# One row at a time for the modulation sums of a fused encoder layer, and nine banks of partial products kept apart by ScalarE

## The chip, the cores and the metric

The kernel runs on one core of a Trainium2 chip. Its time is the device time of one execution in microseconds (us). Before the change three runs gave 939.26, 941.5 and 938.09 us; the median is 939.26 us. The profile comes from a further execution.

## The reference, cut to what matters

One layer (DEPTH is 1) of an encoder over 512 positions of width 2048, in float32:

```python
c_act = silu(c)                                        # 2048 values
mod = c_act @ w_ada + b_ada                            # w_ada is 2048 x 6144
shift, scale, gate = split(mod, 3)
h = rms_norm(x, g) * (1.0 + scale) + shift             # 512 x 2048
proj = h @ w_in                                        # w_in is 2048 x 7168
...                                                    # attention and retention heads on proj
out = y @ w_out
return rms_norm(x + gate * out, final_gain)
```

What matters here is the order that the data force: a column block of h can only be made when the whole 2048-row sum of w_ada for its shift and its scale columns is done, and a row block of w_in can only be multiplied when its column block of h is there.

## The kernel before, in words

**Precision.** Each product is made of three matmuls on halves. `conv` (L170 on) splits a loaded tile of weights: ScalarE casts the high half (L180), VectorE subtracts it to get the low half (L185), both into a tile `w` of three buffers. `mm3` (L94 to L97) then issues high x high, high x low and low x high. h is held the same way, as `hh` and `hl`, transposed (128 of its columns by 512 positions per k).

**The first phase** (L953 to L1032) makes 13 of the units of the projection, 256 columns each: q, k, v, z of the first three attention pairs and one more q. It doesn't wait for all of h. The 16 row blocks k of w_in are cut in six chunks, `CHUNKS = [1, 2, 2, 3, 4, 4]`; this text counts them from 1, so chunk 2 has k = 1, 2, chunk 3 has k = 3, 4, chunk 4 has k = 5, 6, 7, and chunk 5 has k = 8 to 11. In each chunk all 13 units are multiplied with the chunk's k. Two units (`persist`) stay in PSUM all along; of the 11 others each chunk's two banks (pool psA, three banks) are taken out and added up in SBUF: the first chunk by a copy of ScalarE (L992), the later ones by an add of VectorE (L994). In chunk 3 five banks (`MORE`) are copied to tiles of their own by ScalarE instead (L990), and added in chunk 5 (`add_more`, L936). The last unit of a chunk keeps its banks for the next chunk (`keep_now`).

**The modulation sums.** While a chunk is multiplied, the next chunk's columns of w_ada are loaded and summed (`ada_pieces`, L218). The rows come 128 at a time, 16 row blocks in all; a load brings as many of them as fit 2048 elements a partition into a tile `araw` of three buffers. The accumulator, one tile of tag `aacc`, is started by ScalarE with row block 0 (L239) and gets the 15 others by one VectorE instruction each (L243). Then `sums` (L250) transposes it on TensorE into the one bank of pool psM, ScalarE sums each column over the partitions (L278), and VectorE makes shift `sv` and scale `av`. `make_h` (L194) writes for each k the high half `hh` (L197) and the full value `ht` (L202, for chunk 2 on VectorE at L200), both from `xT[k]`; `make_hl` (L204) then subtracts (L211). The tile for `hl` of a chunk has the same tag as that chunk's `xT`, a single buffer, so the first `hl` of a chunk can be written when every `hh` and `ht` of the chunk has been made. `ht` has a tag of its own with four buffers; `aacc` has two.

**The order of the work** is written out by hand. One unit with at most two k is an item: 13 items a chunk for one or two k, 26 for three or four. Items are fed one by one; at feed f (from feed 19 on) the loads of item f are issued, the split of item f-8, and the matmuls and evacuations of item f-10. After each feed the pieces that `agenda` holds for it are issued. `plan` spreads the pieces of the next chunk's sums over the chunk's feeds, from three feeds after its first (`LAG`): first the steps, each of which adds one load's row blocks and starts another load, then `sums`, then each `make_h`, then each `make_hl`. So for chunk 5's sums, planned while chunk 4 is fed, the 20 pieces start at feed 42, the first addition (the fourth piece) at feed 45. The tile framework then orders the instructions of each engine by its own schedule, within the data and buffer dependencies and the extra orders that `after` gives, so pieces can run well ahead of the place where they are issued.

**The last rows of x.** Its 512 rows are normalised and transposed by four row groups. The last group's transposes (`last_rows`, L478) go through psM in four batches issued at feeds 10 to 13, the first taken out by ScalarE, the three others by VectorE (L391). Batches 2 to 4 are k = 5 and up.

Of the kernel before, what the change touches and what calls it, by code (L numbers as in the profile page):

```python
# [17 lines left out]
P = 128  # L18
D = 2048
S = 512  # L20
# [14 lines left out]
UC = 256  # L35
CHUNKS = [1, 2, 2, 3, 4, 4]
N_PERSIST = 2
MORE_AT, MORE = 2, 5
ADA_SPAN = 0.65
TAB_SPAN = 16  # L40
WARM = 4, 1, 1
FIRST_W = OFF_KA + UC
LAG = 3
RAW, RAW1, WB, LOOK, LEAD, LEAD0, LEAD1, EB, YB = 3, 3, 3, 2, 4, 2, 8, 1, 22


# [9 lines left out]
def trunk_kernel(ctx, tc, x, c, norm_gain, w_ada, b_ada, w_in, w_out, dec_f, dec_b, final_gain, out):  # L56
# [116 lines left out]
    def conv(src, n, at, pin_low=None):  # L173
        both = wp.tile([P, 1024 + 128], F32R, tag="w", name="w", bufs=WB)
        hi, lo = both[:, at : at + 512], both[:, at + 512 : at + 1024]
        dh, dl = hi[:, :n], lo[:, :n]
        if len(src.shape) == 3:
            dh = dh.rearrange("p (k f) -> p k f", k=src.shape[1])
            dl = dl.rearrange("p (k f) -> p k f", k=src.shape[1])
        c1 = nc.scalar.copy(dh, src)  # L180
        if pin_low is not None:
            pin_low.append(lambda: pin(nc.vector.tensor_tensor(dl, src, f32(dh), op=ALU.subtract)))
            pin(c1)
            return hi, lo
        c2 = nc.vector.tensor_tensor(dl, src, f32(dh), op=ALU.subtract)  # L185
        marks["split"] = c2
        marks["conv"] = marks.get("conv", 0) + 1
        if marks["conv"] < 3:
            after(c1, marks["hh"])
            after(c2, marks["hl"])  # L190
        return hi, lo


    def make_h(k, nk, k_first):  # L194
        tmp = aap.tile([P, S], F32, tag="ht", name="ht", bufs=4)
        a, b = av[:, k : k + 1], sv[:, k : k + 1]
        ins = nc.scalar.activation(hh[k], xT[k], AF.Identity, scale=a, bias=b)  # L197
        if k_first == 1:
            marks["hh"] = ins
            nc.vector.tensor_scalar(tmp, xT[k], a, b, op0=ALU.mult, op1=ALU.add)  # L200
        else:
            nc.scalar.activation(tmp, xT[k], AF.Identity, scale=a, bias=b)  # L202
        tmps[k] = tmp
# [11 lines left out]
    def h_pieces(k0, nk):  # L215
        return [(lambda f=f, k=k: f(k, nk, k0)) for f in (make_h, make_hl) for k in range(k0, k0 + nk)]

    def ada_pieces(k0, nk):  # L218
        n = nk * P
        acc = aap.tile([P, 2, 4 * P], F32, tag="aacc", name="aacc")  # L220
        npc = 2048 // (2 * n)

        raws = {}

        def load(kr):
            raw = aap.tile([P, 2048], F32, tag="araw", name="araw", bufs=AR)
            rv = raw[:, : npc * 2 * n].rearrange("p (a b f) -> p a b f", a=npc, b=2)
            src = wa[kr * P : (kr + npc) * P, 0 : 2 * D].rearrange(
                "(a p) (b f) -> p a b f", p=P, b=2
            )[:, :, :, k0 * P : k0 * P + n]  # L230
            for b in range(2):
                nc.sync.dma_start(rv[:, :, b], src[:, :, b])
            raws[kr] = rv

        def add(kr):
            rv = raws[kr]
            for a in range(npc):
                if kr + a == 0:
                    first = nc.scalar.activation(acc[:, :, :n], rv[:, a], AF.Copy, scale=ct[:, 0:1])  # L239
                    if k0 in (1, 3):  # L240
                        after(first, marks["hh"])
                else:
                    ins = nc.vector.scalar_tensor_tensor(  # L243
                        acc[:, :, :n], rv[:, a], ct[:, kr + a : kr + a + 1], acc[:, :, :n],
                        op0=ALU.mult, op1=ALU.add,
                    )
                    if k0 in (1, 3) and kr + a == 1:
                        after(ins, marks["hl"])

        def sums():  # L250
            ks = slice(k0, k0 + nk)
            sl = slice(NK + k0, NK + k0 + nk)
            if k0 == 1:
                ps = bank(psM, "psm")
                for b in range(2):
                    for j in range(nk):
                        nc.tensor.matmul(
                            ps[:, b * nk + j : b * nk + j + 1], acc[:, b, j * P : (j + 1) * P], ones[:, 0:1],
                            start=b + j == 0, stop=b + j == nk, skip_group_check=True,
                        )  # L260
                nc.vector.tensor_tensor(sv[:, ks], ps[:, 0:nk], bg[:, ks], op=ALU.add)
                nc.vector.tensor_tensor(av[:, ks], ps[:, nk : 2 * nk], bg[:, sl], op=ALU.add)
                marks["hl"] = nc.vector.tensor_tensor(
                    av[:, ks], av[:, ks], bg[:, 32 + k0 : 32 + k0 + nk], op=ALU.mult
                )
                return
            for b in range(2):
                if b == 0 or nk > 2:
                    ps = bank(psM, "psm")
                    o = 0  # L270
                for j in range(nk):
                    cs = slice(o + j * P, o + (j + 1) * P)
                    nc.tensor.transpose(ps[:, cs], acc[:, b, j * P : (j + 1) * P], ident)
                for j in range(nk):
                    junk = aap.tile([P, P], F32, tag="junk", name="junk")
                    col = b * NK + k0 + j
                    cs = slice(o + j * P, o + (j + 1) * P)
                    nc.scalar.activation(junk, ps[:, cs], AF.Identity, accum_out=md[:, col : col + 1])  # L278
                o += nk * P
            nc.vector.tensor_tensor(sv[:, ks], md[:, ks], bg[:, ks], op=ALU.add)  # L280
            nc.vector.tensor_tensor(av[:, ks], md[:, sl], bg[:, sl], op=ALU.add)
            nc.vector.tensor_tensor(av[:, ks], av[:, ks], bg[:, 32 + k0 : 32 + k0 + nk], op=ALU.mult)

        krs = list(range(0, NK, npc))

        def step(i):
            if i >= AR:
                add(krs[i - AR])
            if i < len(krs):
                load(krs[i])  # L290

        return (
            [(lambda i=i: step(i)) for i in range(len(krs) + AR)]
            + [sums]
            + h_pieces(k0, nk)
        )
# [87 lines left out]
    def evacuated(t, b, eng, late=False):  # L384
        k0, k1 = BANKS[b]
        for i, g in enumerate(groups):
            lo, hi = max(g[0], k0), min(g[-1] + 1, k1)
            if i and lo < hi:
                dst = xt_tiles[i][:, lo - g[0] : hi - g[0], t * P : (t + 1) * P]
                src = psx[t, b][:, (lo - k0) * P : (hi - k0) * P].rearrange("p (k f) -> p k f", k=hi - lo)  # L390
                marks[eng] = eng(dst, src)  # L391
                if not late:
                    pin(marks[eng])

    act, dve = nc.scalar.copy, nc.vector.tensor_copy
    hl[0] = hp.tile([P, 1, S], F32R, tag="g0", name="hl0")[:, 0, :]
    tmp0 = aap.tile([P, S], F32, tag="ht", name="ht", bufs=4)


    def h0_high(cols, src):  # L400
# [78 lines left out]
    def last_rows(b):  # L479
        if b == 1:  # L480
            v = xn[3][:, 1024:D]
            after(nc.vector.tensor_scalar_mul(v, v, rsx[:, 3:4]), marks["sc"])
        turned(3, b, True)
        evacuated(3, b, dve if b else act, True)

    late = [lambda b=b: last_rows(b) for b in range(4)]
    x_scope.close()
# [430 lines left out]
    agenda = {}  # L918
    fed = 0

    for i, f in enumerate(late):
        agenda.setdefault(LEAD1 + LOOK + i, []).append(f)

    def plan(fs, start, span):
        for i, f in enumerate(fs):
            agenda.setdefault(start + (i * span) // len(fs), []).append(f)
# [3 lines left out]
        x3_scope.close()  # L930
        pools["more"] = xn_scope.enter_context(tc.tile_pool(name="more", bufs=1, side="right"))

    agenda.setdefault(LEAD1 + LOOK + len(late), []).append(open_more)
    more = {}

    def add_more(u, i):  # L936
        nc.vector.tensor_tensor(accs[u][i], accs[u][i], more[u, i], op=ALU.add)

    def open_wk():
        xn_scope.close()  # L940
# [12 lines left out]
    for ci, nk in enumerate(CHUNKS):  # L953
# [19 lines left out]
        loose = [u for u in order if u >= N_PERSIST]  # L973
        kept, keep_now = keep_now, {} if lastc else {loose[-1]: None}
        if ci == MORE_AT:
            apart = [(u, i) for u in loose[1:-1:3] for i in range(2)][:MORE]
        if ci == MORE_AT + 2:
            plan([(lambda u=u, i=i: add_more(u, i)) for u, i in apart], fed + 1, 12)
        for u in order:
            mode, c0, ev = ph1[u]  # L980

# [33 lines left out]
        if not lastc:  # L1015
            n2 = CHUNKS[ci + 1]
            nxt = []
            for i in range(0, n2, 4):
                nxt += ada_pieces(k0 + nk + i, min(4, n2 - i))
            before_last = ci == len(CHUNKS) - 2  # L1020
            span = int(len(items) * ADA_SPAN) if before_last else len(items)
            plan(nxt, fed + LAG, span)
            if before_last:
                agenda.setdefault(fed + LAG + span, []).append(open_wk)
        if ci == 0:
# [358 lines left out]
```

## Time and profile before

| | us |
|---|---|
| median of three runs | 939.26 |
| the profiled execution | 940.26 |
| its span, first to last instruction | 938.5 |
| what lies around the span | 1.76 |
| TensorE busy | 920.0 |
| VectorE busy | 619.9 |
| ScalarE busy | 381.0 |

The profile has one line per group of instructions, with the engine, the operation, the tiles as out<-in and the time of one. PE is TensorE's matmuls, PEld its weight loads, DVE is VectorE, ACT is ScalarE, SPq the queue that issues most loads. "idle before" is time in which the engine did nothing before an instruction, with what released it. A windows view gives busy times of the engines for a stretch of the span, with the granted clock of TensorE and what the DMA moved. The chunks can be told apart in the trace by counting matmuls: a unit takes 12 of 128x512, or 24 of 128x256, for two k. Chunk 2 starts at 47.6 us of the span, chunk 3 at 87.1, chunk 4 at 126.9, chunk 5 at 182.8 and chunk 6 at about 255.

### The profile page before, as it was taken

The numbers are of one execution on the slowest core, as the hardware profiler recorded it, in microseconds if no ns is written. First come the engines' busy times: TensorE is split into PE (matmuls) and PEld (weight loads), VectorE is DVE, ScalarE is ACT, GpSimd is POOL, SyncE is SP. The second block draws the span as 40 slices with busy tenths as digits, with TensorE's granted clock in tenths as the row PEclk, the third lists the DMA queues.
The fourth block names the chain that finished last, engine by engine and source line by source line (L and its number), as shares of the span: only waits on it lengthen the run. The fifth ranks groups of instructions, "written<-read, shape, count | busy, mean of one in ns | idle before, by whom it ended". The sixth has DMA issues, their size and how long they took to land.

```text
span 938.5 us, 14336 instructions
## 1 busy us (share of the span) xinstructions
PE 920.0 (98%) x5578; PEld 807.9 (86%) x5578; DVE 619.9 (66%) x1096; ACT 381.0 (41%) x752; POOL 13.7 (1%) x25
## 2 busy tenths in 40 slices
PE   8999999999999999999999999999999999999996
PEld 5787788888988888988998899998899988888896
DVE  4899999959467886666675565845744382546554
ACT  4843525253254655444343232422343372324321
POOL 2000000000000000000000000000000000000001
PEclk9999999999999999999999999999999999999998
DMA  9987988524322222214444534434513148234305
GB/s 329 352 294 259 308 288 281 177 90 127 100 90 67 70 67 70 66 55 136 149 134 146 179 102 158 144 126 158 167 58 112 65 162 290 90 130 140 111 3 180
DMA packets 110244, 141.50 MB, mean 151 GB/s; under 512 B 5800, under 2 KB 81496, under 8 KB 109792
## 3 DMA queue, kind: packets, MB, share of 16 engines
q1 hardware_dynamic: 109072, 137.27, 44.6%
q10 hardware_dynamic: 1008, 3.28, 0.9%
q8 instruction: 44, 0.72, 0.3%
q14 instruction: 24, 0.20, 0.1%
q0 software_dynamic: 96, 0.03, 0.0%
HBM read 136.36 MB, written 4.20 MB: 150 GB/s over the span
## 4 chain that ended last, share of the span: by engine, by line
PE 84%; DVE 7%; DMA 4%; issue 2%; ACT 2%; POOL 0%; SPq 0%; POOLq 0%; DVEq 0%; ACTq 0%
PE pp L97 24%; PE pw L97 12%; PE pp L95 12%; PE po L97 12%; PE pw L95 6%; PE po L95 6%; DVE aacc L243 3%; PE op L97 3%; DMA araw<-in_w_ada_dram 2%; PE sp L97 2%; PE op L95 2%; PE tp L799 1%; DMA raw<-in_w_ada_dram 1%; DVE w L185 1%; PE sp L95 1%
## 5 line engine op out<-in xcount | busy, mean ns | idle before, releaser
L185 DVE TENSOR_TENSOR w<-raw,w 128x512 fp32r<-128x512 f32 (+1 forms) x288 | 193.6, 673 | 214.8 <-ACT w L180 214.5
L180 ACT CAST w<-raw 128x512 fp32r<-128x512 f32 (+1 forms) x289 | 174.7, 606 | 390.5 <-PE pp L97 187.1
L95 PE MATMUL pp<-w,hh 128*128 128x256 f32 x576 | 160.2, 278 | 0.0
L97 PE MATMUL pp<-w,hh 128*128 128x256 f32 x576 | 159.7, 277 | 0.0
L97 PE MATMUL pp<-w,hl 128*128 128x256 f32 x576 | 159.7, 277 | 0.0
L95 PEld LDWEIGHTS pp<-w,hh 128*128 128x128 f32 x576 | 108.4, 188 | 1.0 <-issue 0.2
L97 PEld LDWEIGHTS pp<-w,hh 128*128 128x128 f32 x576 | 108.3, 188 | 0.9
L97 PEld LDWEIGHTS pp<-w,hl 128*128 128x128 f32 x576 | 108.2, 188 | 0.0
L95 PE MATMUL pw<-hh,w 128*128 128x512 f32 x256 | 101.5, 397 | 3.4 <-DVE acc L994 2.1
L95 PE MATMUL pp<-hh,w 128*128 128x512 f32 x256 | 99.8, 392 | 0.4 <-DVE kl L699 0.4
L97 PE MATMUL pw<-hh,w 128*128 128x512 f32 x256 | 100.0, 391 | 0.1
L97 PE MATMUL pp<-hl,w 128*128 128x512 f32 x256 | 100.0, 391 | 0.0
L97 PE MATMUL pp<-hh,w 128*128 128x512 f32 x256 | 99.9, 390 | 0.0
L97 PE MATMUL pw<-hl,w 128*128 128x512 f32 x256 | 99.7, 391 | 0.0
L97 PE MATMUL po<-w,yh 128*128 128x512 f32 (+1 forms) x252 | 91.1, 361 | 0.0
L95 PE MATMUL po<-w,yh 128*128 128x512 f32 (+1 forms) x252 | 91.0, 361 | 0.0
L97 PE MATMUL po<-w,yl 128*128 128x512 f32 (+1 forms) x252 | 91.0, 361 | 0.0
L243 DVE SCALAR_TENSOR_TENSOR aacc<-araw,ct,aacc 128x512 f32<-128x512 f32 (+2 forms) x75 | 76.4, 1018 | 5.6 <-DMA araw<-in_w_ada_dram 2.9
L994 DVE TENSOR_TENSOR acc<-acc,pw 128x512 f32<-128x512 f32 x95 | 63.5, 686 | 4.6 <-PE pw L97 4.1
L95 PEld LDWEIGHTS pw<-hh,w 128*128 128x128 f32 x256 | 48.1, 188 | 17.2 <-DVE acc L994 4.7
L95 PEld LDWEIGHTS pp<-hh,w 128*128 128x128 f32 x256 | 48.0, 188 | 10.8 <-DVE kl L699 0.8
L97 PEld LDWEIGHTS pw<-hh,w 128*128 128x128 f32 x256 | 48.1, 188 | 10.6 <-DVE w L185 0.5
(237 smaller groups left out, 1568.6 us busy)
## 6 DMA issues: line engine op xcount, KB each, us to landing
raw<-in_w_in_dram SPq DMA_DIRECT2D x94, 512.0 KB, 3.6
araw<-in_w_ada_dram SPq DMA_DIRECT2D x48, 512.0 KB, 6.8
graw<-in_w_ada_dram SPq DMA_DIRECT2D x64, 256.0 KB, 3.0
raw<-in_w_out_dram SPq DMA_DIRECT2D x32, 512.0 KB, 3.7
raw<-in_w_in_dram SPq DMA_DIRECT2D x16, 384.0 KB, 4.1
araw<-in_w_ada_dram SPq DMA_DIRECT2D x16, 384.0 KB, 4.3
res<-in_x_dram SPq DMA_DIRECT2D x16, 256.0 KB, 6.2
raw<-in_w_in_dram SPq DMA_DIRECT2D x11, 256.0 KB, 5.1
```

The source lines that it names most:

```text
L95: nc.tensor.matmul(o, lh, rh, start=start, stop=False, skip_group_check=True)
L97: nc.tensor.matmul(o, a, b, start=False, stop=stop and b is (rl if swap else rh), skip_group_check=True)
L180: c1 = nc.scalar.copy(dh, src)
L185: c2 = nc.vector.tensor_tensor(dl, src, f32(dh), op=ALU.subtract)
L243: ins = nc.vector.scalar_tensor_tensor(acc[:, :, :n], rv[:, a], ct[:, kr + a : kr + a + 1], acc[:, :, :n], op0=ALU.mult, op1=ALU.add,)
L799: nc.tensor.transpose(tp_[:, j * P : (j + 1) * P], pt[:, j * P : (j + 1) * P], ident)
L994: nc.vector.tensor_tensor(accs[u][i], accs[u][i], ps[i], op=ALU.add)
```

## The change

It has five parts. In chunks 2 and 3 the pieces of the next chunk's sums are no longer spread evenly: each row block is a piece of its own (`row`), placed by a share of the chunk's items (`ENDS`), and each addition is ordered behind the split before the latest one issued (`marks["prev"]`). `ht` loses its tag: two `ht` share one tile of tag `aacc`, and the accumulator is asked for at its first addition. `MORE` goes from five banks to nine, one bank of each of nine units, and their adds in chunk 5 are spread over 27 feeds and ordered behind the latest split. The last rows of x go to feeds 10, 23, 25 and 27, and are all taken out by ScalarE. `tmp0`, a temporary of the first k, moves to the pool x3p.

```diff
-MORE_AT, MORE = 2, 5
+MORE_AT, MORE = 2, 9
+LATE = 10, 23, 25, 27
+ENDS = {1: (0.72, 0.86), 2: (0.68, 0.82)}
...
-        marks["split"] = c2
+        marks["prev"], marks["split"] = marks.get("split", c2), c2
...
     def make_h(k, nk, k_first):
-        tmp = aap.tile([P, S], F32, tag="ht", name="ht", bufs=4)
+        if (k - k_first) % 2 == 0:
+            tmps["pair"] = aap.tile([P, 2, 4 * P], F32, tag="aacc", name="ht")
+        tmp = tmps["pair"][:, (k - k_first) % 2, :]
...
-    def ada_pieces(k0, nk):
+    def ada_pieces(k0, nk, ends=None):
         n = nk * P
-        acc = aap.tile([P, 2, 4 * P], F32, tag="aacc", name="aacc")
+        accw = {}
...
-        def add(kr):
+        def add(kr, only=None):
             rv = raws[kr]
-            for a in range(npc):
+            for a in range(npc) if only is None else [only]:
+                if kr + a == 0:
+                    accw["t"] = aap.tile([P, 2, 4 * P], F32, tag="aacc", name="aacc")
+                acc = accw["t"]
...
+                    if only is not None:
+                        after(ins, marks["prev"])
...
+        def row(r):
+            add(krs[r // npc], r % npc)
+            if r % npc == npc - 1 and r // npc + AR < len(krs):
+                load(krs[r // npc + AR])
+        if ends:
+            n_items, rows_end, h_end = ends
+            at = [i - 5 for i in range(AR)] + [r * rows_end * n_items / NK - 0.5 for r in range(NK)]
+            fs = [lambda i=i: load(krs[i]) for i in range(AR)] + [lambda r=r: row(r) for r in range(NK)]
+            hs = h_pieces(k0, nk)
+            s = (rows_end + 0.04) * n_items
+            at += [s] + [s + 0.3 + (h_end * n_items - s) * j / len(hs) for j in range(len(hs))]
+            return list(zip(at, fs + [sums] + hs))
...
-    tmp0 = aap.tile([P, S], F32, tag="ht", name="ht", bufs=4)
+    tmp0 = x3p.tile([P, S], F32, name="ht0")
...
-        evacuated(3, b, dve if b else act, True)
+        evacuated(3, b, act, True)
...
-    for i, f in enumerate(late):
-        agenda.setdefault(LEAD1 + LOOK + i, []).append(f)
+    for at, f in zip(LATE, late):
+        agenda.setdefault(at, []).append(f)
...
     def add_more(u, i):
-        nc.vector.tensor_tensor(accs[u][i], accs[u][i], more[u, i], op=ALU.add)
+        after(nc.vector.tensor_tensor(accs[u][i], accs[u][i], more[u, i], op=ALU.add), marks["split"])
...
-            apart = [(u, i) for u in loose[1:-1:3] for i in range(2)][:MORE]
+            apart = [(u, 0) for u in loose[1 : 1 + MORE]]
-            plan([(lambda u=u, i=i: add_more(u, i)) for u, i in apart], fed + 1, 12)
+            plan([(lambda u=u, i=i: add_more(u, i)) for u, i in apart], fed + 1, 3 * MORE)
...
+            if ends:
+                for at, f in nxt:
+                    agenda.setdefault(fed + LEAD1 + LOOK + math.floor(at), []).append(f)
+            else:
+                plan(nxt, fed + LAG, span)
```

More of the change, by code (lines that the diff above doesn't have):

```diff
@@ L250, in sums @@
         def sums():
+            acc = accw["t"]
             ks = slice(k0, k0 + nk)
@@ L931, in open_more @@
         pools["more"] = xn_scope.enter_context(tc.tile_pool(name="more", bufs=1, side="right"))
-    agenda.setdefault(LEAD1 + LOOK + len(late), []).append(open_more)
+    agenda.setdefault(LATE[-1] + 1, []).append(open_more)
     more = {}
     def add_more(u, i):
-        nc.vector.tensor_tensor(accs[u][i], accs[u][i], more[u, i], op=ALU.add)
+        after(nc.vector.tensor_tensor(accs[u][i], accs[u][i], more[u, i], op=ALU.add), marks["split"])
     def open_wk():
@@ L1017, in trunk_kernel @@
             nxt = []
+            ends = ENDS.get(ci)
             for i in range(0, n2, 4):
-                nxt += ada_pieces(k0 + nk + i, min(4, n2 - i))
+                nxt += ada_pieces(k0 + nk + i, min(4, n2 - i), ends and (len(items), *ends))
             before_last = ci == len(CHUNKS) - 2
             span = int(len(items) * ADA_SPAN) if before_last else len(items)
-            plan(nxt, fed + LAG, span)
+            if ends:
[3 more added lines that the diff above has]
+                plan(nxt, fed + LAG, span)
             if before_last:
```

## The prediction, made before the change was run

> **What bounds the kernel now.** I read the page first, then TensorE by stages, then the waits of the worst stage.
>
> ```profile
> span 938.5 us, 14336 instructions
> PE 920.0 (98%) x5578; PEld 807.9 (86%) x5578; DVE 619.9 (66%) x1096; ACT 381.0 (41%) x752; POOL 13.7 (1%) x25
> DVE  4899999959467886666675565845744382546554
> GB/s 329 352 294 259 308 288 281 177 90 127 100 90 67 70 67 70 66 55 136 149 134 146 179 102 158 144 126 158 167 58 112 65 162 290 90 130 140 111 3 180
> ```
>
> TensorE is busy for 920.0 of 938.5 us, so only a few us of waits can be won. VectorE's slices say where: 9s from about 45 to 190 us, while h is still being made. After that TensorE is the bound and the change touches nothing.
>
> ```profile
> core 0: us, PE busy (x) PEld busy (x) DVE busy (x) ACT busy (x) POOL busy (x), PEclk, DMA share, GB/s
> 47.60:62.00 14.40, 14.40 (x103) 13.32 (x102) 14.04 (x23) 4.71 (x8) 0.00 (x0) 1.00 0.95 321
> 62.00:112.60 50.60, 46.81 (x205) 36.48 (x204) 48.51 (x75) 24.20 (x53) 0.00 (x0) 1.00 0.83 274
> 112.60:126.90 14.30, 14.14 (x97) 12.94 (x96) 14.06 (x19) 2.89 (x5) 0.00 (x0) 1.00 0.76 249
> 126.90:182.80 55.90, 55.22 (x298) 46.96 (x297) 52.45 (x76) 22.27 (x51) 0.00 (x0) 1.00 0.78 266
> 182.80:255.00 72.20, 72.20 (x393) 62.51 (x392) 50.70 (x98) 25.68 (x54) 0.88 (x1) 1.00 0.33 103
> 160.00:190.00 30.00, 30.00 (x134) 24.75 (x133) 29.88 (x44) 7.63 (x14) 0.00 (x0) 1.00 0.51 163
> ```
>
> The last row is the yardstick: TensorE waits for nothing and starts 134 matmuls of 128x512 in 30 us, one in 0.224 us, so an item of 12 takes 2.69 us. The second row holds the last eight items of chunk 2 and the first eight of chunk 3, all of this form:
>
> ```profile
> L95 PE MATMUL pw<-hh,w 128*128 128x512 f32 x64 | 25.7, 402 | 2.3 <-DVE acc L994 1.5 <-ACT more L990 0.7
> L97 PE MATMUL pw<-hl,w 128*128 128x512 f32 x64 | 25.1, 392 | 0.0
> L97 PE MATMUL pw<-hh,w 128*128 128x512 f32 x64 | 24.9, 392 | 0.0
> L273 PE MATMUL psm<-ident,aacc 128*128 128x128 f32 x10 | 1.9, 284 | 1.5 <-ACT junk L278 1.5
> ```
>
> That is 192 matmuls, 43.0 us at the yardstick, in 50.6 us. About 0.7 us of the 7.6 us between go to the ten transposes (I put them at 0.07 us each, as they overlap); **6.9 us are waits**, though PE's busy time shows only 3.8 us of idleness, since a started matmul counts as busy past the next one's start. The waits say for whom, in the same window:
>
> ```profile
> PEld pw L95 <- DVE acc L994: 3.3, 4, 1.1
> PEld psm L273 <- ACT junk L278: 2.3, 2, 1.9
> PEld pw L95 <- ACT more L990: 1.1, 1, 1.1
> ACT aacc L239 <- DMA araw<-in_w_ada_dram: 4.5, 2, 3.2
> ```
>
> Banks wait for VectorE's adds, which stand behind w_ada rows, and ScalarE stood 3.2 us before a first row whose load was late. [...]
>
> **Row by row, and nine banks.** VectorE's prices:
>
> ```profile
> L185 DVE TENSOR_TENSOR w<-raw,w 128x512 fp32r<-128x512 f32 x270 | 186.1, 690 | 214.4 <-ACT w L180 214.2
> L994 DVE TENSOR_TENSOR acc<-acc,pw 128x512 f32<-128x512 f32 x95 | 63.5, 686 | 4.6 <-PE pw L97 4.1
> L243 DVE SCALAR_TENSOR_TENSOR aacc<-araw,ct,aacc 128x1024 f32<-128x1024 f32 x30 | 38.5, 1283 | 3.1 <-DMA araw<-in_w_ada_dram 2.9
> L243 DVE SCALAR_TENSOR_TENSOR aacc<-araw,ct,aacc 128x768 f32<-128x768 f32 x15 | 15.4, 1027 | 0.0
> L211 DVE TENSOR_TENSOR hl<-ht,hh 128x512 fp32r<-128x512 f32 x15 | 9.6, 686 | 0.0
> L202 ACT ACTIVATE ht<-xT,sv,av 128x512 f32<-128x512 f32 x13 | 10.5, 804 | 0.0
> L992 ACT COPY acc<-pw 128x512 f32<-128x512 f32 x22 | 12.2, 608 | 1.3 <-PE pw L97 1.1
> ```
>
> Four more banks by ScalarE take 4 x 0.686 = 2.7 us off VectorE in chunk 3; three copies of x less take about 2 us (my estimate from L994's length) off it in chunk 2. ScalarE gets 7 x 0.608 = 4.3 us, beside 24.20 of 50.6 us busy: hidden. The four adds come back in chunk 5, where VectorE has 50.70 of 72.2 us: hidden, and 2.7 us if that cover were gone. Pinning each row behind a split lets a bank wait for one row, not for several. The loads that `row` issues go through SP's queue in turn with w_in's, which are issued eight items ahead and can stand a wait there: 0. Of the 6.9 us I count 5 as won; the bounds are 0 (nothing moves, as rows alone still fill VectorE) and 6.9. What is late next is the late junk, which sits behind ScalarE's first rows.
>
> **Last rows of x, tmp0.** Batches 2 to 4 now run in gaps that TensorE has anyway:
>
> ```profile
> 44.59 1.05 PE L257 MATMUL psm<-ones,aacc 128*128 128x1 f32 x8 [0.15 <-DVE aacc L243]
> 46.05 0.52 PE L380 MATMUL psx<-ident,xt 128*128 128x128 f32 x3 [0.41 <-DVE av L262]
> 47.23 0.66 PE L380 MATMUL psx<-ident,xt 128*128 128x128 f32 x4 [0.65 <-DVE xT L391]
> ```
>
> The wait until 47.6 us stays, as chunk 2's first `hh` ends it, not the batches. Moved into chunk 2 they cost what they take there: two batches, seven transposes, 0.5 to 1 us; I take 0.6. `tmp0` moves storage only: 0.
>
> **The shared buffers.** This decides. The second transpose row shows the rule of a buffer: its batch needs psM's bank, and waits for `av` L262, the last reader of the sums that held it. Now `aacc`, with two buffers, serves the accumulators and the pairs of `ht`. Let me walk the feeds around chunk 4. Chunk 3's first item is 26, so with (0.68, 0.82) and 13 items `sums` is at 26 + 10 + floor(9.36) = feed 45, `make_h` of k = 5 and 6 at floor(9.66) and floor(9.88), also 45, and of k = 7 at floor(10.09), feed 46. But chunk 5's sums are planned from feed 42 and make their first addition, which now asks for the accumulator, at feed 45, behind k = 6 and ahead of k = 7. So tiles are asked for in this order: accumulator of chunk 4, pair (5, 6), accumulator of chunk 5, then k = 7. As I read the pools, tiles of one tag are given out in the order asked, each when a buffer's last reader is done. The pair (5, 6) takes the buffer of (3, 4), the accumulator of chunk 5 that of chunk 4, and `ht` of 7 must wait for one of them. The pair can't come first: its reader `hl` of 5 goes into the buffer of xT of k = 5 to 7, which `make_h` of 7 still reads. So it waits **until all 16 row blocks of chunk 5 are added and transposed**, and `hl` of 5, without which chunk 4 can't pass its first high x high products, waits behind it.
>
> The price. Before, those rows ran beside chunks 3 and 4:
>
> ```profile
> 100.22 1.15 ACT L239 ACTIVATE aacc<-araw,ct 128x1024 f32<-128x1024 f32 x1 [3.20 <-DMA araw<-in_w_ada_dram]
> 137.19 1.28 DVE L243 SCALAR_TENSOR_TENSOR aacc<-araw,ct,aacc 128x1024 f32<-128x1024 f32 x1
> 144.36 0.27 ACT L278 ACTIVATE junk<-psm 128x128 f32<-128x128 f32 x1
> 146.31 0.28 ACT L278 ACTIVATE junk<-psm 128x128 f32<-128x128 f32 x1 [0.81 <-PE psm L273]
> ```
>
> After: chunk 3 starts near 84.6 (half of the 5 us won by then, beside 0.6), so item 35, ahead of `sums`, ends at 84.6 + 10 x 2.7 = 111.6. The chunk's sums read its accumulator at about 111 and the next starts: 1.15 on ScalarE, 15 x 1.28 = 19.2 on VectorE, 6.8 for the splits and adds of chunk 3's last four items: 138.2. Loads set a like bound: 16 blocks of 0.52 MB (128 partitions of 1024 numbers) at 340 GB/s, near the page's highest slice of 352, are 25 us, part of it fetched before. Then 1.95 us from the first half's transposes to the second's (144.36 to 146.31), 0.80 for `ht`, 0.69 for `hl`, about 0.4 of hand-overs: chunk 4 goes on at 142. It could have started at 122.5 (126.9 - 5 + 0.6), so TensorE stands about 19.5 us, less 0.9 for high products done ahead. Against before: 142 - 126.9 - 0.9 = +14.2 us. Chunk 4 then runs freely, its transposes done in the pause: of its 55.9 us the yardstick asks 52.5, and I take 2 back.
>
> **Sum**: +14.2 - 2 = +12.2 us on a span of 938.5, that is 950.7; the profiled execution lay 1.76 above its span and 1.0 above the median, so 939.26 + 12.2 = **951.5 us**. The size hangs on when the rows end: 131 if they start at 107 and meet free loads (+5, 944), 146 if each takes 1.9 us as with the chunk's own loads beside (+20, 959).
>
> **The rivals.** *No pause, faster.* If a buffer goes to whoever is ready first, or k = 7 is served ahead, `ht` of 7 follows `sums` at once, and only the gains count: -5 + 0.6 = -4.4, 935 us, from 931 (all 6.9 and chunk 4's 2) to 940. For it speaks that the schedule does reorder: at 100.22 a first row runs before the earlier chunk's sums. Against it, reordering an instruction isn't reordering who holds a buffer. It decides as soon as `ht` of 7 stands ahead of the next accumulator. *A short pause.* If the accumulator's loads come at once and the gains are whole, rows end near 128 and the time is within 4 us of before: about 940. For it, buffers of `araw` come free from feed 41 on; against it, 15 x 1.28 us can't shrink. *Late h of chunk 3.* Its `make_h` now comes at feeds 33 and 34, two or three items before use; `sums`, four ScalarE passes of 0.8 and two subtractions take 6 us of these 8. It costs where the rows run over 2 us late: +2 on gains of 5, 937 to 941. [...]
>
> **How the numbers follow.** The pause 0.80, no pause 0.14, the two others 0.03 each. I count as the same what lies within 0.5% (4.7 us), about what a measurement of this kernel can tell. The pause gives slower, but for 0.01; no pause splits 0.09 faster and 0.05 same; the two others are 0.04 same, 0.02 slower. So faster 0.09, same 0.10, slower 0.81. The range runs from 941 to 959: the pause's own bounds, and below it the short pause, with no pause left out.
>
> **What would show it.** In the changed profile: an idle stretch of TensorE of 15 to 22 us near 122, ended by `hl` L211 of k = 5; ScalarE's `ht` of 7 right behind the junk of chunk 5's sums; rows of 128x1024 running alone on VectorE in that stretch; before it, waits for `acc` below 2 us. If `ht` of 7 stands ahead of the first 128x1024 row, I am wrong, and the time is near 935.

## The result, and the profile after

The changed kernel takes 960.59 us (median of four runs, 959.34 to 961.84), beside 938.99 us of the kernel before: a ratio of 1.0223, with a 95% interval of 1.0207 to 1.0240. It is slower by 21.6 us; 951.5 was forecast, with a range to 959. The direction was right, the size was not.

Five lines of the page of the changed kernel, to be held against those of before:

```profile
span 960.1 us, 14343 instructions
PE 923.1 (96%) x5578; PEld 811.8 (85%) x5578; DVE 621.8 (65%) x1093; ACT 385.5 (40%) x759; POOL 12.5 (1%) x25
PE   8999918999999999999999999999999999999996
DVE  4888784986688787666875574665554473537454
PEclk9999967999999999999999999999999999999999
```

and two of the page of before:

```profile
PE   8999999999999999999999999999999999999996
PEclk9999999999999999999999999999999999999998
```

The busy times are those of before within 5 us, so the 21.6 us that were added are not more work. Of VectorE's 9s up to 190 us only the last is left, from 168 to 192 us; the others have gone to 8 and less. And there is a new thing: in the slice from 120 to 144 us TensorE is busy for a tenth of the time, and in that slice and the next its granted clock is 0.6 and 0.7. The next step is to find the chunk. Counted by matmuls, in the same way for both kernels (so 0.1 to 0.3 us ahead of the starts named earlier), the chunks end at (differences are taken before rounding):

| end of | before | changed | difference |
|---|---|---|---|
| chunk 2 | 86.8 | 86.3 | -0.6 |
| chunk 3 | 126.8 | 122.8 | -3.9 |
| chunk 4 | 182.7 | 204.2 | +21.5 |
| chunk 5 | 255.1 | 276.7 | +21.5 |
| the span | 938.5 | 960.1 | +21.6 |

All is lost in chunk 4. Its windows in the changed kernel (the columns are as in the windows view of before):

```profile
122.80:149.20 26.40, 3.82 (x14) 2.10 (x12) 20.21 (x21) 3.58 (x18) 0.00 (x0) 0.58 0.94 332
149.20:154.50 5.30, 5.28 (x13) 4.14 (x14) 1.57 (x5) 2.39 (x7) 0.00 (x0) 0.50 0.02 7
154.50:204.20 49.70, 49.70 (x273) 43.33 (x272) 45.09 (x65) 17.47 (x31) 0.00 (x0) 1.00 0.58 185
```

For 26.4 us TensorE does almost nothing, then it works for 5.3 us at half its clock, then it runs as it should. Its timeline says what ended each stretch (start, duration, then the instruction, with the idle time before it and what ended that in brackets):

```profile
123.92 0.73 PE L98 MATMUL pp<-hh,w 128*128 128x512 f32 x2 [0.26 <-ACT w L183]
144.07 1.11 PE L287 MATMUL psm<-ident,aacc 128*128 128x128 f32 x4 [19.43 <-DVE aacc L253]
146.48 1.11 PE L287 MATMUL psm<-ident,aacc 128*128 128x128 f32 x4 [1.29 <-ACT junk L292]
149.22 0.80 PE L100 MATMUL pp<-hl,w 128*128 128x512 f32 x1 [1.63 <-DVE hl L217]
...
150.24 0.63 PE L98 MATMUL pp<-hh,w 128*128 128x512 f32 x1
...
154.72 0.39 PE L98 MATMUL pp<-hh,w 128*128 128x512 f32 x1
```

TensorE waits for the last row of chunk 5's sums, transposes them, and gets `hl` of k = 5 only then. ScalarE's timeline shows why that `hl` is late:

```profile
119.68 0.80 ACT L208 ACTIVATE ht<-xT,sv,av 128x512 f32<-128x512 f32 x1
120.39 1.14 ACT L249 ACTIVATE aacc<-araw,ct 128x1024 f32<-128x1024 f32 x1
121.43 0.80 ACT L203 ACTIVATE hh<-xT,sv,av 128x512 fp32r<-128x512 f32 x1
...
147.63 0.81 ACT L208 ACTIVATE ht<-xT,sv,av 128x512 f32<-128x512 f32 x1 [1.21 <-PE psm L287]
```

`hh` of k = 7 is made at 121.43, and `ht` of k = 7, which needs the same inputs and a buffer, at 147.63, right after the sums of chunk 5 have left theirs. VectorE's timeline, of the rows between:

```profile
121.56 1.28 DVE L253 SCALAR_TENSOR_TENSOR aacc<-araw,ct,aacc 128x1024 f32<-128x1024 f32 x1 [4.05 <-ACT aacc L249]
...
136.06 7.96 DVE L253 SCALAR_TENSOR_TENSOR aacc<-araw,ct,aacc 128x1024 f32<-128x1024 f32 x6 [1.18 <-DMA araw<-in_w_ada_dram]
...
148.48 1.90 DVE L217 TENSOR_TENSOR hl<-ht,hh 128x512 fp32r<-128x512 f32 x3 [1.86 <-ACT ht L208]
```

The rows start at 121.56, where the forecast had them start at 112, and the first `hl` follows at 148.48.

### The profile page after: what moved, and what is told of

Same layout as the page of the kernel before. It is cut to its first block, busy times and chain, and to the rows that moved or that the text cites. A ratio compares the mean times of both kernels' runs of the same rounds, so it can differ in the third digit from the quotient of the medians.

```text
span 960.1 us, 14343 instructions
## 1 busy us (share of the span) xinstructions
PE 923.1 (96%) x5578; PEld 811.8 (85%) x5578; DVE 621.8 (65%) x1093; ACT 385.5 (40%) x759; POOL 12.5 (1%) x25
## 4 chain that ended last, share of the span: by engine, by line
PE 91%; DVE 3%; DMA 2%; ACT 1%; issue 1%; POOL 0%; SPq 0%; POOLq 0%; DVEq 0%; ACTq 0%
PE pp L100 24%; PE pw L100 17%; PE pp L98 12%; PE po L100 12%; PE pw L98 8%; PE po L98 6%; PE op L100 3%; PE sp L100 2%; DVE aacc L253 2%; PE op L98 2%; PE tp L828 1%; DMA raw<-in_w_ada_dram 1%; PE sp L98 1%; PE psa L358 1%; DMA araw<-in_w_ada_dram 1%
## 5 line engine op out<-in xcount | busy, mean ns | idle before, releaser
L98 PE MATMUL pp<-hh,w 128*128 128x512 f32 x256 | 100.9, 397 | 0.7 <-DVE kl L728 0.4
L100 PE MATMUL pp<-hh,w 128*128 128x512 f32 x256 | 101.2, 395 | 0.0
L1024 DVE TENSOR_TENSOR acc<-acc,pw 128x512 f32<-128x512 f32 x91 | 61.2, 683 | 9.4 <-PE pw L100 8.8
L100 PEld LDWEIGHTS pp<-hl,w 128*128 128x128 f32 x256 | 49.1, 192 | 12.3 <-DVE hl L217 2.0
L98 PEld LDWEIGHTS pw<-hh,w 128*128 128x128 f32 x256 | 48.1, 188 | 11.4 <-ACT hh L430 0.8
```

The lines of the kernel that those rows point to most:

```text
L98: nc.tensor.matmul(o, lh, rh, start=start, stop=False, skip_group_check=True)
L100: nc.tensor.matmul(o, a, b, start=False, stop=stop and b is (rl if swap else rh), skip_group_check=True)
L1024: nc.vector.tensor_tensor(accs[u][i], accs[u][i], ps[i], op=ALU.add)
```

## The experiments

The theory (A): `ht` of k = 7 asks for a buffer of `aacc` behind the accumulator of chunk 5, gets it when that accumulator is done, and the pause lasts until then. Its rivals: (B) the rows of 128x1024 cost VectorE 20 us wherever they stand, and the new places have pushed them into the open; (C) two buffers for two uses cost time in any order. The kernel before was timed again beside them: its median was 940.14 us beside the first four experiments, 939.57 us beside half the rows, three buffers, the old last rows and the first filling of the pause, and 939.24 us beside the rest. The ratios are to those runs, and differ by up to 0.0007 from the quotient of the two medians.

**k = 7 first.** One number, by which `make_h` of k = 7 comes at feed 45 and so ahead of the accumulator:

```diff
-ENDS = {1: (0.72, 0.86), 2: (0.68, 0.82)}
+ENDS = {1: (0.72, 0.86), 2: (0.68, 0.78)}
```

> The changed kernel with one number altered: the pieces of chunk 4's h end at 0.78 of the chunk and not at 0.82, so that make_h of k = 7 is issued at feed 45, ahead of the accumulator of chunk 5, and not at feed 46 behind it. Theory A (the order in which the buffers of aacc are asked for makes the pause): no idle stretch of TensorE near 124, no granted clock of 0.50 near 150, ht of 7 ahead of the first 128x1024 row; the changed kernel is ahead of the one before by 3.9 us when chunk 3 ends, so 939 - 3.9 = 935 us, 932 to 938. Theory B (16 rows of 128x1024 cost 22 us of VectorE wherever they stand, and moving one piece only moves them): 950 to 960 us. Theory C (sharing two buffers costs in any order, since pairs and accumulators wait for each other): a shorter pause somewhere, 942 to 950 us.

Measured: 940.48 us, ratio 1.0001 (0.9991 to 1.0010). The pause is gone, and B with it. But 935 wasn't reached either: chunk 3 ends at 122.8, 4.0 us ahead of before, and chunk 4 at 183.3, 0.6 us behind. The accumulator is started on ScalarE and the rows on VectorE like this:

```profile
123.26 1.15 ACT L249 ACTIVATE aacc<-araw,ct 128x1024 f32<-128x1024 f32 x1 [0.59 <-ACT w L183]
```

```profile
124.64 1.28 DVE L253 SCALAR_TENSOR_TENSOR aacc<-araw,ct,aacc 128x1024 f32<-128x1024 f32 x1
```

Before, the first such row ran at 103.83. Now the accumulator is behind both pairs, its 16 rows are packed into the first half of chunk 4, and there VectorE is the bound again; a window of that stretch, and the waits from 130 to 160 us:

```profile
140.00:150.00 10.00, 6.81 (x49) 5.78 (x49) 9.48 (x12) 2.05 (x4) 0.00 (x0) 1.00 0.99 333
```

```profile
PEld pw L100 <- DVE w L188: 2.9, 2, 1.7
...
PEld pw L98 <- DVE acc L1024: 1.5, 2, 1.1
```

So C holds in a small way: with the rows in their new places the kernel that shares gives back, even in the right order, what the rows won. That the sharing does it is read from the late start of the accumulator; the nine banks stand beside it in this kernel.

**`ht` in its own tag.**

```diff
-MORE_AT, MORE = 2, 9
+MORE_AT, MORE = 2, 5
...
-        if (k - k_first) % 2 == 0:
-            tmps["pair"] = aap.tile([P, 2, 4 * P], F32, tag="aacc", name="ht")
-        tmp = tmps["pair"][:, (k - k_first) % 2, :]
+        tmp = aap.tile([P, S], F32, tag="ht", name="ht", bufs=4)
...
-    tmp0 = x3p.tile([P, S], F32, name="ht0")
+    tmp0 = aap.tile([P, S], F32, tag="ht", name="ht", bufs=4)
```

> The changed kernel with ht back in a tag of its own with four buffers (and tmp0 with it); five banks instead of nine, as the memory doesn't hold both. All feeds stay, make_h of k = 7 still at feed 46 behind the accumulator of chunk 5. Theory A: with nothing to wait for, ht of 7 runs right behind the sums of chunk 4; no pause; 934 to 939 us. Theory B: the pause stays, 950 to 960 us. Theory C: no pause either, 934 to 939 us.

Measured: 935.77 us, ratio 0.9949 (0.9934 to 0.9964). The feeds are those of the changed kernel; the buffer isn't shared, four banks fewer are kept apart, and the pause is gone. The four banks can't be what removed it: the kernel above keeps nine and has no pause either. The first 128x1024 row now runs at 114.35, and chunk 4 takes 56.1 us (121.1 to 177.2), as before:

```profile
114.35 1.28 DVE L251 SCALAR_TENSOR_TENSOR aacc<-araw,ct,aacc 128x1024 f32<-128x1024 f32 x1
```

**The shared buffers alone, in the kernel before,** by the same lines as above the other way round, with the accumulator asked for at its first addition:

```diff
-        acc = aap.tile([P, 2, 4 * P], F32, tag="aacc", name="aacc")
+        accw = {}
...
+                if kr + a == 0:
+                    accw["t"] = aap.tile([P, 2, 4 * P], F32, tag="aacc", name="aacc")
+                acc = accw["t"]
...
+            acc = accw["t"]
```

> The kernel before with the shared buffers alone: ht in pairs of tag aacc, the accumulator asked for at its first addition, tmp0 in x3p; rows, banks and last rows as before. Here make_h of k = 7 is issued at feed 39, ahead of the accumulator of chunk 5 at feed 45. Theory A: no pause, 936 to 943 us, about the 939 of before (an accumulator may start a few us later). Theory B: 939 us. Theory C: 944 to 955 us, with stretches of 5 us and more in which TensorE waits for ht or aacc.

Measured: 940.03 us, ratio 0.9997 (0.9987 to 1.0006). In the order that the old places give, the sharing costs nothing that can be measured.

**The same, with k = 7 put off.**

```diff
-            plan(nxt, fed + LAG, span)
+            if ci == 2:
+                plan(nxt[:-4], fed + LAG, span - 4)
+                plan(nxt[-4:], fed + LAG + span + 4, 2)
+            else:
+                plan(nxt, fed + LAG, span)
```

> The kernel with the shared buffers alone, and in it make_h of k = 7 (with the three subtractions for hl behind it) put off to feed 46, behind the accumulator of chunk 5 at feed 45; the pieces ahead of it end four feeds earlier. Rows, banks and last rows as before. Theory A: the pause is there without the rest of the change: TensorE idle for 15 to 25 us in chunk 4's first items, ended by hl of 5, the clock at 0.50 behind it; 955 to 965 us. Theories B and C: four h pieces two to seven feeds later cost at most what h comes too late, 1 to 4 us over the kernel with the shared buffers alone.

Measured: 958.39 us, ratio 1.0187 (1.0172 to 1.0202): 18.4 us over the last kernel, by putting four pieces off (and ending the others four feeds earlier). ScalarE's timeline has the same signature as the changed kernel's:

```profile
108.88 1.16 ACT L244 ACTIVATE aacc<-araw,ct 128x1024 f32<-128x1024 f32 x1
...
143.94 0.81 ACT L204 ACTIVATE ht<-xT,sv,av 128x512 f32<-128x512 f32 x1 [1.21 <-PE psm L279]
```

With these four the cause is shown both ways: the sharing without the order makes no pause, the order without the sharing makes none, and both together make it, with or without the rest of the change.

**What sets the length: half the rows.**

```diff
-                else:
+                elif k0 != 8 or kr + a < 8:
                     ins = nc.vector.scalar_tensor_tensor(
```

> The changed kernel without the additions of row blocks 8 to 15 of chunk 5's sums (left out; their loads stay). Theory A (the pause lasts until chunk 5's rows are added and transposed): eight additions of 1.28 us less and their two waits of 1.5 us for a load partly with them, so that the pause ends 10 to 12 us earlier: 949 to 951 us. Rival (the pause ends with something else, such as the loads of w_in that stand behind those of w_ada): 957 to 961 us.

Measured: 948.93 us, ratio 1.0093 (1.0080 to 1.0106), 11.7 us less than the changed kernel. This kernel leaves out half of the sum, so it doesn't compute the layer; it serves for the time alone. The first `hl` comes at 136.06 and not at 148.48. The rows set the end of the pause.

**What sets the length: the rows started earlier.**

```diff
-                plan(nxt, fed + LAG, span)
+                plan(nxt, fed + (2 if ci == 3 else LAG), span)
```

> The changed kernel with the pieces of chunk 5's sums planned one feed earlier (two feeds after the chunk's first and not three), so that its accumulator is asked for at feed 44, ahead of the pair (5, 6) at 45 and of k = 7 at 46. The accumulator then takes the buffer of the pair (3, 4), free since 86, and needn't stand behind ScalarE's passes for k = 5 and 6; ht of 7 must still wait for chunk 5's sums. Theory A (the pause ends when 16 rows have been added, so it ends earlier by as much as they start earlier): the first 128x1024 row at 110 to 114 and not at 121.6, the pause shorter by 6 to 10 us, 951 to 955 us. Rival (the loads set the end of the rows, whose 16 blocks need 25 us at the 340 GB/s of the pause, and they aren't started earlier): 957 to 961 us.

Measured: 954.33 us, ratio 1.0161 (1.0144 to 1.0178). VectorE's first row, and its `hl`:

```profile
110.55 1.28 DVE L253 SCALAR_TENSOR_TENSOR aacc<-araw,ct,aacc 128x1024 f32<-128x1024 f32 x1
...
133.92 2.60 DVE L253 SCALAR_TENSOR_TENSOR aacc<-araw,ct,aacc 128x1024 f32<-128x1024 f32 x2 [1.23 <-DMA araw<-in_w_ada_dram]
140.99 1.90 DVE L217 TENSOR_TENSOR hl<-ht,hh 128x512 fp32r<-128x512 f32 x3 [1.85 <-ACT ht L208]
```

The rows start 11.0 us earlier, the pause ends 7.5 us earlier. Of both, 1.9 us come from chunk 3, which ends that much earlier in this execution (122.8 and 120.9; the last section says why), so the pause itself is 5.6 us shorter, a little less than the 6 to 10 expected. The rows now share VectorE with chunk 3's last splits and adds, and wait 2.9 us for loads, where they waited 1.5. So the start of the rows and the loads both have a part in it, and the start has the larger one.

**Three buffers** instead of two, in the changed kernel's own order:

```diff
-MORE_AT, MORE = 2, 9
+MORE_AT, MORE = 2, 7
...
-            tmps["pair"] = aap.tile([P, 2, 4 * P], F32, tag="aacc", name="ht")
+            tmps["pair"] = aap.tile([P, 2, 4 * P], F32, tag="aacc", name="ht", bufs=3)
```

(and `bufs=3` at the two other tiles of that tag).

> The changed kernel with three buffers of tag aacc instead of two, and seven banks instead of nine to make room. The order of asking is the changed kernel's: pair (5, 6), accumulator of chunk 5, then the pair of k = 7, which now finds a free buffer. Theory A: no pause; 935 us if chunk 5's rows also start as early as with ht in a tag of its own (114 of the span), 937 to 941 us if they start as late as with k = 7 first (124). Theory B (placing alone): 955 us and more.

Measured: 937.90 us, ratio 0.9976 (0.9966 to 0.9986), no pause, first row at 118.67. Three kernels now line up by the start of chunk 5's rows: 114.4, 118.7 and 124.6 us, with a chunk 4 of 56.1, 58.6 and 60.5 us. They also differ in their banks (5, 7 and 9), but those are copied in chunk 3 and added in chunk 5; that the start of the rows sets the length is argued from the three, and wasn't tested alone.

**Where the gain is from.** Three kernels with `ht` in its own tag and five banks. The first is the one with `ht` in its own tag, and puts the last rows of x back (feeds 10 to 13, three batches by VectorE):

```diff
-LATE = 10, 23, 25, 27
+LATE = 10, 11, 12, 13
...
-        evacuated(3, b, act, True)
+        evacuated(3, b, dve if b else act, True)
```

> The kernel with ht in a tag of its own and five banks (935.8 us), and in it the last rows of x as before: feeds 10 to 13, three batches taken out by VectorE. What stays of the change is rows one at a time and five banks of five different units. If the last rows' move is what brought the 2.3 us that this kernel was ahead at the end of chunk 2: 938 us. If rows and banks bring the gain: 935.5 to 936.5 us.

Measured: 935.77 us, ratio 0.9962 (0.9948 to 0.9975), so the gain isn't that of the last rows' move. The second has the old choice of banks and the old adds as well:

```diff
-        after(nc.vector.tensor_tensor(accs[u][i], accs[u][i], more[u, i], op=ALU.add), marks["split"])
+        nc.vector.tensor_tensor(accs[u][i], accs[u][i], more[u, i], op=ALU.add)
...
-            apart = [(u, 0) for u in loose[1 : 1 + MORE]]
+            apart = [(u, i) for u in loose[1:-1:3] for i in range(2)][:MORE]
...
-            plan([(lambda u=u, i=i: add_more(u, i)) for u, i in apart], fed + 1, 3 * MORE)
+            plan([(lambda u=u, i=i: add_more(u, i)) for u, i in apart], fed + 1, 12)
```

> The kernel before with the rows alone: ENDS, a row block a piece, each ordered behind a split, the accumulator asked for at its first addition; ht in its own tag, the five banks and their adds as before, the last rows of x as before. The kernel that has also one bank of each of five units and the spread adds took 935.8 us. If the rows bring the gain: 935 to 937 us. If the spread of the banks brings it: 938 to 940 us.

Measured: 936.12 us, ratio 0.9965 (0.9952 to 0.9978). The third is the kernel before with the new choice of five banks and the spread adds, that is, the last diff the other way round:

> The kernel before with the banks alone: still five, but one of each of five units, their adds spread over 15 feeds of chunk 5 and ordered behind a split. If the rows bring the gain: 939 to 940 us, as before. If the banks bring it: 935 to 937 us.

Measured: 939.48 us, ratio 1.0004 (0.9995 to 1.0013). The waits of TensorE for `acc` in chunks 2 and 3 (from 62 us to 109 with the rows alone, to 111 with the banks alone) say the same; first the rows, then the banks:

```profile
PEld pw L98 <- DVE acc L1022: 0.2, 1, 0.2
```

```profile
PEld pw L95 <- DVE acc L994: 2.9, 3, 1.2
```

The rows bring the whole gain, 3 to 4 us. The new choice of five banks brings none: in its one profile chunk 3 ends 1.3 us ahead of before, but the median of its eleven runs isn't ahead. Nine banks in memory of their own were in no run. What the traces show of them is the end of chunk 3: 120.9 us with nine (in the kernel with the rows ahead), 121.1 us with five (with `ht` in its own tag).

**What the restart costs: the pause filled.** Matmuls whose result is overwritten keep TensorE at work in the pause:

```diff
+                    if k0 == 8 and b == 0:
+                        for i in range(80):
+                            nc.tensor.matmul(ps, hh[7][:, 0:P], hh[7], start=True, stop=True, skip_group_check=True)
```

> The changed kernel with 80 matmuls of 128x512 (both operands from hh of k = 7, into the bank that the transposes of chunk 5's sums overwrite) issued right ahead of those transposes, so that TensorE works through the pause; 80 at 0.226 us are 18.1 of the 19.7 us between the last high product and the first transpose. Nothing else is altered. Theory A (the idleness lowers TensorE's clock, and the restart is paid for at 0.50): clock 1.00 throughout, the four transposes in 0.5 us and not in 1.11, the first dozen matmuls at 0.23 us and not at 0.43; 3 to 4 us less, 956.5 to 958 us. Rival (the clock falls for another reason, or the restart costs nothing that isn't hidden): 960 to 961 us.

Measured: 960.45 us, ratio 1.0218 (1.0199 to 1.0238). They ran out at 142, the rows ended at 145.3, and the clock fell before the restart: the first four transposes, at 145.33, took 0.66 us, the next four, at 147.27, 1.11. So 94 were tried instead of 80:

> The changed kernel with 94 matmuls of 128x512 in the pause instead of 80. With 80 they ran out 3.3 us ahead of the first transpose, and the clock fell all the same. 94 at 0.227 us reach from 124.3 to 145.6, up to or just over the end of the rows; behind them stand 4 us in which only eight transposes run. If the idleness lowers the clock and this is short enough: clock 1.00, the restart's matmuls at 0.23 us, 957 to 959 us. If those 4 us are enough to lower it, or the restart's low clock costs nothing on the path: 960 to 962 us.

Measured: 960.67 us, ratio 1.0223 (1.0206 to 1.0240). The windows:

```profile
118.00:144.00 26.00, 25.63 (x113) 20.73 (x111) 20.39 (x18) 3.78 (x6) 0.00 (x0) 1.00 0.83 287
144.00:149.00 5.00, 1.85 (x10) 1.32 (x11) 1.62 (x5) 2.98 (x17) 0.00 (x0) 1.00 0.85 290
149.00:152.50 3.50, 3.50 (x10) 2.70 (x9) 0.84 (x4) 1.52 (x2) 0.00 (x0) 0.53 0.01 4
```

The clock was held through the pause (1.00), and the four transposes took 0.66 us and not 1.11. But behind the next 5 us, of which TensorE worked for 1.85, it was 0.53. In this execution the rows also began 1.9 us earlier and ended no earlier, with 3.6 us of waits for loads. So neither median shows the price of the low clock. The traces do, side by side: these kernels restart with different lengths of half clock (in all five the matmuls of 128x512 start 0.43 us apart in it, and 0.23 us apart behind it), and what is left of chunk 4 is the same work in each.

| kernel (all in us) | first low product (`hl` x high) at | at half clock from there | from there to the end of chunk 4 | less half of the time at half clock |
|---|---|---|---|---|
| changed | 149.2 | 5.2 | 55.0 | 52.3 |
| rows ahead | 141.7 | 3.7 | 54.3 | 52.4 |
| 80 matmuls | 150.0 | 3.6 | 54.2 | 52.4 |
| 94 matmuls | 148.5 | 3.4 | 54.1 | 52.4 |
| shared alone, k = 7 put off | 145.5 | 4.1 | 54.4 | 52.4 |

The last column is the same within 0.1 us in all five, 0.9 us above the 51.5 that the yardstick asks for the 230 matmuls that are left. So nothing hides the restart: half of the time at half clock is lost, 2.6 us in the changed kernel.

## Why the prediction was wrong

**The mechanism was right**, to the instruction: the shared buffers, the order of feeds 45 and 46, `ht` of k = 7 behind chunk 5's sums, `hl` of 5 behind it, TensorE's stretch without work from 124.6 (24.6 us with only eight transposes in them, where 15 to 22 had been named). The pause had 0.80. The rival that put reordered instructions against buffers, no pause, is refuted by the changed kernel and by the kernel with k = 7 put off.

**The step that failed** is the start of the rows: "The chunk's sums read its accumulator at about 111 and the next starts: 1.15 on ScalarE". It puts the first row on VectorE at 112.2; it ran at 121.56, 9.4 us later. About 5 of these are the accumulator: chunk 3 began 1.7 us later than I had it (the clock of 0.72 from 47 to 53 us that the last section describes; where it stayed at 1.00, in the kernel with the rows ahead, it began at the 84.6 of the forecast), its own last row ran at 110.93 and ended at 111.9, and its transposes came in two halves through one bank, the second until about 116. The other 4 are ScalarE: the last `junk`, two `hh` and two `ht` were issued ahead of the first row, which came at 120.39. I had counted ScalarE's passes for k = 5 and 6 nowhere ahead of the rows, though my own list of the order of asking had the pair in front. The kernel with the rows ahead tests this term: there they begin at 110.55, TensorE goes on at 141.7, where the forecast had 142, and the time is 954.3. That 141.7 meets 142 is in part luck: the rows begin 1.7 us before the forecast's 112.2 and take its 26.0, and the step from the last row to the first low product takes 5.2 us and not 3.8.

**A term that was missing** is the restart. The sum took TensorE to go on at full speed. In the changed kernel twelve matmuls from 149.22 to 154.49 take 5.3 us, which at the yardstick's 0.224 are 2.7, and the eight transposes ran at half the clock too (0.50 from 144 to 149): four take 1.11 us, and 0.66 us where 94 matmuls filled the pause.

**The sum, remade**: forecast +12.2. Rows begin 9.4 later; they take 22.5 us and not 26.0, since three splits and 1.5 us of waits for loads stood among them, and not the 6.8 us of splits and adds that I had put there (-3.5); from the last row to the first low product 5.15 us and not 3.8 (+1.35); chunk 4 from there on 55.0 us and not 53.0 (+2.0), the restart's 2.6 less 0.6 that was won beyond the 2 forecast. That makes +21.4 of the measured 21.6. The range ended at 959 by rows that end at 146; they ended at 144.0, and the two terms at half the clock, 2.6 and 0.9 us, carried the time over it. The steps to that bound aren't given: 112.2 + 15 x 1.9 is 140.7, or 147.5 with the 6.8, which would have made the end of the range 960.8. Nor are those to the lower one, 131.

**The gain.** Forecast -4.4 by the end of chunk 3, measured -3.9. By the mechanism it was larger: kernels with the same rows in which the clock stays at 1.00 near 50 us (below) end chunk 3 at 120.9 to 121.4, 5.3 to 5.9 us ahead of before, so of the 6.9 us of waits most were won. No wait of TensorE for `acc` is left from 62 to 112.6 us, as forecast. The rows won it; the four more banks, priced at 2.7 us of VectorE in chunk 3, moved the end of chunk 3 by no more than 0.2 us (120.9 with nine, 121.1 with five).

**The small terms.** The late batches, 0.6: at the end of chunk 2 the kernel with them is 0.7 us behind the one without (84.5 and 83.8), and at the end of chunk 3 no longer (121.1 and 121.3). The size was right by luck, as the cost stands in another place: only the last batch moved into chunk 2 (its four transposes run at 61.9 us), seven transposes stay ahead of it, and chunk 2 itself begins 0.7 us later (48.1 and 47.4). Of that, 0.4 us stand already in the matmuls of the sums ahead of the batches (44.8 and 44.4); the rest fits ScalarE's copy of a batch, which at 46.83 is now right ahead of the chunk's first `hh` at 47.20. `tmp0`, 0, stands. Late h of chunk 3 didn't happen: its `hl` are made from 83.8 on, and chunk 3 starts at 86.3.

## What to carry to other kernels

When two uses share the buffers of one tag, write down in which order they ask, and look for a pair in which the later asker is needed sooner: here it stopped TensorE for 24.6 us in a stage of 56, and one number in a schedule makes it or removes it. Price such a wait from the moment when the first instruction of the blocking work can really issue, with all that stands ahead of it on its engine, and add the restart, 2.6 us here. And before memory is freed for something, measure what can be had without it: here the rows with five banks and unshared buffers take 935.8 us, better than both kernels, and no run shows a gain of the nine banks that asked for the memory.

## What the runs showed of the hardware

In the pause of the changed kernel TensorE's clock fell, and it came back late: TensorE is idle from 124.6, its mean clock is 0.71 from 125 to 130 and 0.50 from 130 on, and it is at 1.00 again only from 154.5, 5.3 us after the restart. With the pause filled by 94 matmuls it stayed at 1.00 up to 144. In some of the profiles a low clock also came behind a much shorter stretch with waits. Between 45 and 48 us each of these kernels has the same two short waits around seven transposes (TensorE is busy for 1.97 of these 3 us in the changed kernel), and in the stretch from 47 to 53 us six of fourteen profiles show a mean clock of 0.72, the others 1.00; first the changed kernel, then the one with the rows ahead, whose rows up to there are the same in the trace but for 0.1 us:

```profile
47.00:53.00 6.00, 5.65 (x21) 4.57 (x22) 4.97 (x8) 2.73 (x5) 0.00 (x0) 0.72 1.08 355
```

```profile
47.00:53.00 6.00, 5.73 (x28) 4.70 (x29) 4.97 (x9) 3.29 (x6) 0.00 (x0) 1.00 1.08 353
```

That is 21 matmuls against 28, and 1.7 us lost (0.28 of 6 us); it is most of the 1.9 us by which the changed kernel is less far ahead at the end of chunk 3 than that one. The low clock of the changed kernel lies in one stretch:

```profile
48.64:52.05 3.41, 3.41 (x12) 2.83 (x11) 3.30 (x5) 1.09 (x3) 0.00 (x0) 0.50 1.09 356
```

This stretch at half clock (0.50) is 3.4 us long, and half of it is the 1.7 us. The 3.4 us ahead of it weren't idle: the seven transposes and the first matmuls of chunk 2 ran in them. Why the clock is low here in six of the profiles and not in the others was not shown.
